# One-hot sets of i: half of them from a table product and ScalarE instead of a VectorE comparison

## The chip, the core and the metric

The kernel runs on one core of a Trainium2 chip. A core has TensorE (PE, matrix products), VectorE (DVE), ScalarE (ACT), GpSimd (POOL) and SyncE (SP, which here issues transfers), and 16 DMA engines that all queues share. The metric is device time in microseconds (us) of one execution, median over runs.

## What is computed

One encoder layer over 1024 tokens of width 1024: attention and a Hyena mixer, a layer norm, and then a PEER feed-forward, which alone matters here. Each token picks, per head, 16 of 128 x 128 experts by the sums of two top-16 lists, and adds the experts' rows up:

```
q = (xc @ w_q).reshape(C, PEER_HEADS, 2, PEER_DK // 2)
s = jnp.einsum('chpd,hpnd->chpn', q, sub_keys, ...)
sv, si = lax.top_k(s, PEER_TOPK)
cand = sv[:, :, 0, :, None] + sv[:, :, 1, None, :]
cidx = si[:, :, 0, :, None] * PEER_NKEYS + si[:, :, 1, None, :]
best, pos = lax.top_k(cand, PEER_TOPK)
eidx = take_along_axis(cidx, pos)
g = softmax(best)
a = gelu(einsum('chkd,cd->chk', u_tab[eidx], xc))
out = einsum('chk,chkd->cd', g * a, v_tab[eidx])
```

An expert's number is 128 i + j, with i and j from 0 to 127.

## The kernel before

The 1024 tokens are eight tiles of 128. Three of them (group 0 to 2) are done by **gathers**: GpSimd fetches the picked rows of peer_u and peer_v by indirect transfers (`grow`, L1249, 128 rows of 4 KB each time, 384 for u and 384 for v), and VectorE makes the dot product of a u row (L1262) or adds a v row up (`gacc`, L1270). Six buffers `grow` go round, so a gather waits for VectorE to have used the row of six before.

The other five tiles are done **densely**: for each of the 128 values of i, TensorE multiplies all 128 experts of that i with the 640 tokens. I call this an expert block. `u_load` fetches the block's table `ur` (512 KB, one buffer), ScalarE rounds it to `uh` (L291) and VectorE makes the rest `ul` (L292), each with two buffers; `u_part` then makes 48 products of 320 columns (L285 to L287) in two banks `ps_x`, and ScalarE takes the gelu of them (L1221) into `A`, which goes to memory in the first 72 blocks (EARLY). Later, `weigh` reads `A` back, multiplies it by the weights `gt`, and `v_group` multiplies by peer_v (`vh`, `vl`): that needs all weights first. So the 72 early blocks and what makes the weights run side by side, and the first v product ends this stage.

Making the weights of a dense tile has two parts. `route` does the top-k lists and finds i, j and the softmax weight, nearly all of it on VectorE; at its end the numbers go through memory (`jx_d`) and come back as `jl`, with tokens along the free side. `build_g` then has 32 steps a tile (160 in all), each for four tokens (NB). A step makes, for each token, a set of one-hots of i (`p1`, a comparison of `iota` with `ig` on VectorE, L1160) and a set of one-hots of j times the weight (`p2`). `p2` comes from a table product, `parabola`: a matmul of `jl` with the constant table `par_r` gives 1-(j-j')^2 in a bank `ps_o` (L1153), and a Relu on ScalarE with the weight as scale leaves the weight where j = j' and zero elsewhere (L1166, one instruction a token). Four matmuls of 128 x 128 a step multiply `p2` by `p1` (L1183; I call them hots), ScalarE copies the result (L1184), and each eight steps go to memory as 2 MB.

The code is written as generators. `weights()` interleaves `route` and `build_g`, and the loop over EARLY takes from it in proportion to the blocks written (`total / GFILL`). The gathers are taken by `tick`. The order on each engine is then chosen by a scheduler from what is ready; only instructions that share buffers are bound to the written order: a pool gives its buffers out in turn, in the order in which the code asks for them. `psX` has four banks, `psH` two, `psO` two (`ps_o0`, `ps_o1`). Before the change only `u_part` asks for banks of `psX` in this stage.

Of the kernel before, what the change touches and what calls it, by code (L numbers as in the profile page):

```python
# [10 lines left out]
F32 = mybir.dt.float32  # L11
F32R = mybir.dt.float32r
BF16 = mybir.dt.bfloat16
I32 = mybir.dt.int32
U32 = mybir.dt.uint32
AF = mybir.ActivationFunctionType
ALU = mybir.AluOpType
# [4 lines left out]
P = 128  # L22
T = 1024
D = 1024
NT = T // P
# [270 lines left out]
def layer(ctx: ExitStack, tc: tile.TileContext, a: dict, out: bass.AP):  # L296
    nc = tc.nc
# [9 lines left out]
    dram = ctx.enter_context(tc.tile_pool(name="dram", bufs=1, space=DRAM))  # L307
# [55 lines left out]
    psX = s_ps.enter_context(tc.tile_pool(name="psX", bufs=4, space=PSUM))  # L363
    psH = s_ps.enter_context(tc.tile_pool(name="psH", bufs=2, space=PSUM))
    psO = s_ps.enter_context(tc.tile_pool(name="psO", bufs=1, space=PSUM))

    def bank():
        return psX.tile([P, 512], F32, name="ps_x")
# [177 lines left out]
    with tc.tile_pool(name="rqp", bufs=1, side="right") as rqp:  # L546
# [4 lines left out]
        for cts, ones in (((0, 1), ones_q), ((2,), ones_kv)):  # L551
# [6 lines left out]
            r = rqp.tile([P, T], F32, name="r")  # L558
# [7 lines left out]
    for j in (*range(4, 12), *range(4)):  # L566
# [5 lines left out]
                                       op0=ALU.mult, op1=ALU.add)  # L572
        nc.vector.scalar_tensor_tensor(y[:, 0:T - 1], u[:, 1:T], sw[:, j, 2:3], y[:, 0:T - 1],
                                       op0=ALU.mult, op1=ALU.add)
# [158 lines left out]
    with tc.tile_pool(name="ltp", bufs=2, side="right") as ltp:  # L733
# [70 lines left out]
        for c in range(2):  # L804
# [6 lines left out]
            for tt in range(0, NT, 2):  # L811
                ps = bank()
                for e in range(2):
                    s = slice((tt + e) * P, (tt + e + 1) * P)
# [110 lines left out]
    iota = keep.tile([P, P], F32, name="iota")  # L925
# [89 lines left out]
    def route(tt, rp, done):  # L1015


        s = rp.tile([P, 16, P], F32, name="r_s")
# [50 lines left out]
        w = rp.tile([P, 8, 16], F32, name="r_w")  # L1069
# [12 lines left out]
        nc.vector.tensor_mul(w, w, den_b)  # L1082
        ei = rp.tile([P, P], I32, name="r_ei")
        nc.vector.tensor_copy(ei, ef2)
        ij = rp.tile([P, 2, P], I32, name="r_ij")
        nc.vector.tensor_scalar(ij[:, 0], ei, 7, None, op0=ALU.arith_shift_right)
        nc.vector.tensor_scalar(ij[:, 1], ei, 127, None, op0=ALU.bitwise_and)
        ijf = rp.tile([P, P], F32, name="r_ijf")
        nc.vector.tensor_copy(ijf, ij[:, 0])
        jj = rp.tile([P, P], I32, name="r_jj")  # L1090
        nc.vector.tensor_tensor(jj, ij[:, 1], ij[:, 1], op=ALU.mult)
        jp = rp.tile([P, 2, P], I32, name="r_jp")
        nc.vector.tensor_scalar(jp[:, 1], jj, 127, None, op0=ALU.bitwise_and)
        nc.vector.tensor_scalar(jp[:, 0], jj, 127 << 7, None, op0=ALU.bitwise_and)
        jx = rp.tile([P, 3, P], BF16, name="r_jx")
        nc.vector.tensor_copy(jx[:, 0], ij[:, 1])
        nc.vector.tensor_copy(jx[:, 1:3], jp)
        nc.sync.dma_start(jx_d[tt].rearrange("r t s -> t r s"), jx)
        jl = jls[tt % 2]
        for r in range(3):  # L1100
            nc.sync.dma_start(jl[32 * r:32 * r + 32], jx_d[tt, r].rearrange("(q t) s -> t q s", t=32))
        ps = psO.tile([P, 2, P], F32, name="ps_o0")
        nc.tensor.transpose(ps[:, 0], ijf, ident)
        nc.tensor.transpose(ps[:, 1], w.rearrange("p h k -> p (h k)"), ident)
        ig = rp.tile([P, 2, P], F32, name="ig", bufs=2)
# [28 lines left out]
    CS = 32  # L1134
    GI = 4
    NCS = TD // CS
    jx_d = dram.tile([NT, 3, P, P], BF16, name="jx_d")
    NB = 4
    HOT = 0.69
    g_d = dram.tile([NCS, P, P, CS], F32, name="g_d")  # L1140
# [1 line left out]
    def build_g(ijg, t, gp):  # L1142


        ig, jl = ijg
        steps = [(cs, c4) for cs in range(P // CS) for c4 in range(0, CS, NB)]
        par, hot = {}, {}

        def parabola(n):
            cs, c4 = steps[n]  # L1150
            ps = psO.tile([P, NB, P], F32, name=f"ps_o{n % 2}")
            c = cs * CS + c4
            nc.tensor.matmul(ps, jl[0:98, c // 32], par_r[0:98, c % 32:c % 32 + NB], start=True, stop=True)  # L1153
            par[n] = ps

        def hots(n):
            cs, c4 = steps[n]
            c = cs * CS + c4
            p1 = gp.tile([P, NB, P], F32, name="p1", bufs=4)
            nc.vector.tensor_tensor(p1, iota.unsqueeze(1).to_broadcast([P, NB, P]),  # L1160
                                    ig[:, 0, c:c + NB].unsqueeze(2).to_broadcast([P, NB, P]),
                                    op=ALU.is_equal)
            p2 = gp.tile([P, NB, P], F32, name="p2", bufs=4)
            ps = par.pop(n)
            for j in range(NB):
                nc.scalar.activation(p2[:, j], ps[:, j], AF.Relu, scale=ig[:, 1, c + j:c + j + 1])  # L1166
            hot[n] = p1, p2

        with tc.issue_after(ended[-1]) if ended else ExitStack():
            parabola(0)  # L1170
            parabola(1)
        hots(0)
        for n, (cs, c4) in enumerate(steps):
            if n + 2 < len(steps):
                parabola(n + 2)
            if n + 1 < len(steps):
                hots(n + 1)
            if c4 == 0:
                st = gp.tile([P, P, CS], F32, name="gst", bufs=2)
            p1, p2 = hot.pop(n)  # L1180
            ps = psH.tile([P, NB, P], F32, name="ps_h")
            for j in range(NB):
                nc.tensor.matmul(ps[:, j], p2[:, j], p1[:, j], start=True, stop=True)  # L1183
            nc.scalar.copy(st[:, :, c4:c4 + NB], ps.rearrange("p c i -> p i c"))  # L1184
            if c4 + NB == CS:
                nc.scalar.dma_start(g_d[t * (P // CS) + cs], st)
            yield HOT
# [20 lines left out]
    def u_part(i, psum):  # L1208

        for n in (i, i + 1):  # L1210
            if n < P and n not in ready:
                u_load(n)
        uh, ul = ready.pop(i)
        A = up.tile([P, TD], F32, name="A", bufs=3)
        for c in range(2):
            s = slice(c * HT, (c + 1) * HT)
            ps = psum()
            for ct in range(ND):
                r = mm3(nc, ps, (uh[:, ct], ul[:, ct]), (hd[:, 0, ct, s], hd[:, 1, ct, s]),
                        ct == 0, ct == ND - 1)  # L1220
            nc.scalar.activation(A[:, s], ps, AF.Gelu)  # L1221
        ended.append(r.ins)
        return A
# [71 lines left out]
    def tick(cost):  # L1295
        pace["credit"] += cost
        while pace["credit"] >= pace["step"]:
            pace["credit"] -= pace["step"]
            next(ga, None)
# [5 lines left out]
    with tc.tile_pool(name="rp", bufs=1, side="left") as rp, \  # L1305
            tc.tile_pool(name="gp", bufs=1, side="left") as gp:
        base = gp.tile([98, P], F32, name="base")
        own = gp.tile([98, 32], F32, name="own")
        nc.sync.dma_start(base, a["par_base"])
        nc.sync.dma_start(own, a["par_own"])  # L1310
        par_r = gp.tile([98, 32, P], BF16, name="par_r")
        nc.vector.tensor_mul(par_r, base.unsqueeze(1).to_broadcast([98, 32, P]),
                             own.unsqueeze(2).to_broadcast([98, 32, P]))
        jls = [gp.tile([98, 4, P], BF16, name=f"jl{i}") for i in range(2)]
        for jl in jls:
            nc.gpsimd.memset(jl[96:98], 1.0)
        r0 = route(0, rp, [])
        for _ in scores(hd, NG, DENSE):
            with tc.issue_after(normed[-1].ins):
                for _ in range(2):  # L1320
                    next(r0, None)
        for _ in r0:
            pass
        s_q.close()
        gap = s_e.enter_context(tc.tile_pool(name="gap", bufs=2, side="right"))

        def weights():


            done = []  # L1330
            yield from route(NG, rp, done)
            for t in range(DENSE):
                beside = route(NG + t + 1, rp, done) if t + 1 < DENSE else route(1, rp, done)
                for n, c in enumerate(build_g(done[t], t, gp)):
                    yield c
                    if n % 5 in (0, 2, 4):
                        yield next(beside, 0.0)
                yield from beside
            for g in range(2, NG):
                yield from route(g, rp, done)  # L1340

        gw = weights()
        total = (NT - 1) * 12 * CHUNK + TD // NB * HOT
        done = 0.0
        for e in range(EARLY):
            while done < (e + 1) * total / GFILL:
                c = next(gw, None)
                if c is None:
                    break
                done += c  # L1350
            A = u_part(e, u_early)
            nc.scalar.dma_start(a_d[e], A)
            tick(UC)
        for _ in gw:
            pass
# [199 lines left out]
```

## Time and profile before

| | |
|---|---|
| three runs | 3267.38 us median (3263.86 to 3277.91) |
| the profiled execution | 3255.75 us, span 3254.0 us |
| TensorE busy | 2988.5 us (92%) |
| VectorE busy | 2735.7 us (84%) |
| ScalarE busy | 1256.2 us (39%) |
| GpSimd busy | 1036.4 us (32%) |

Busy time is the union of an engine's instructions. A matmul's recorded length covers the length of its pipeline, and the next one starts well before its end, so a busy TensorE is not a full one: its true load is read from the distance of starts. Idle time of an engine matters only where others wait for it.

### The profile page before, as it was taken

The numbers are of one execution on the slowest core, as the hardware profiler recorded it, in microseconds if no ns is written. First come the engines' busy times: TensorE is split into PE (matmuls) and PEld (weight loads), VectorE is DVE, ScalarE is ACT, GpSimd is POOL, SyncE is SP. The second block draws the span as 40 slices with busy tenths as digits, with TensorE's granted clock in tenths as the row PEclk, the third lists the DMA queues.
The fourth block names the chain that finished last, engine by engine and source line by source line (L and its number), as shares of the span: only waits on it lengthen the run. The fifth ranks groups of instructions, "written<-read, shape, count | busy, mean of one in ns | idle before, by whom it ended". The sixth has DMA issues, their size and how long they took to land.

```text
span 3254.0 us, 44798 instructions
## 1 busy us (share of the span) xinstructions
PE 2988.5 (92%) x15582; PEld 2552.1 (78%) x15582; DVE 2735.7 (84%) x5514; ACT 1256.2 (39%) x2454; POOL 1036.4 (32%) x797
## 2 busy tenths in 40 slices
PE   6999898889999779999999789998999999799997
PEld 5677676556689778999898778886888888588886
DVE  7556799888757799999999768888889879888888
ACT  4544344455523216766574122222222222122222
POOL 0000000000000351332435735555555445455551
PEclk9999889989999989999999899999999999999998
DMA  5244743322444777887888999999999999989995
GB/s 173 97 149 133 249 123 104 102 56 73 138 152 149 278 252 241 302 303 277 310 284 319 364 338 336 325 358 341 329 358 323 353 315 333 337 302 353 342 332 188
DMA packets 355064, 828.87 MB, mean 255 GB/s; under 512 B 34345, under 2 KB 144851, under 8 KB 351253
## 3 DMA queue, kind: packets, MB, share of 16 engines
q0 software_dynamic: 110592, 402.70, 34.5%
q1 hardware_dynamic: 230709, 356.71, 33.9%
q10 hardware_dynamic: 13536, 66.59, 5.2%
q8 instruction: 123, 2.02, 0.2%
q14 instruction: 104, 0.85, 0.1%
HBM read 715.52 MB, written 110.33 MB: 254 GB/s over the span
## 4 chain that ended last, share of the span: by engine, by line
PE 31%; DVE 22%; DMA 7%; issue 6%; POOL 3%; ACT 1%; SPq 0%; DVEq 0%; POOLq 0%; ACTq 0%
PE ps_x L285 5%; PE ps_x L287 5%; PE ps_x L286 5%; DVE grow L1262 4%; DVE gacc L1270 4%; DMA vr<-in_peer_v 3%; PE ps_h L285 3%; PE ps_h L287 3%; PE ps_h L286 3%; POOL grow L1249 3%; DVE p L1160 2%; PE ps_o L285 2%; PE ps_o L286 2%; PE ps_o L287 2%; DVE ul L292 2%
## 5 line engine op out<-in xcount | busy, mean ns | idle before, releaser
L1249 POOL DMA_INDIRECT grow<-in_peer_u,eid x384 | 518.0, 1349 | 582.3 <-DVE grow L1262 206.9
L1249 POOL DMA_INDIRECT grow<-in_peer_v,eid x384 | 504.8, 1315 | 606.1 <-DVE gacc L1270 267.3
L1270 DVE SCALAR_TENSOR_TENSOR gacc<-grow,dot,gacc 128x1024 f32<-128x1024 f32 x381 | 487.3, 1279 | 13.2 <-DMA grow<-in_peer_v,eid 9.6
L1262 DVE SCALAR_TENSOR_TENSOR grow<-grow,gh 128x1024 f32<-128x1024 f32 x384 | 460.1, 1218 | 19.8 <-DMA grow<-in_peer_u,eid 19.5
L287 PE MATMUL ps_x<-hd,ul 128*128 128x320 f32 x1152 | 368.3, 328 | 50.1 <-DVE ul L292 49.7
L285 PE MATMUL ps_x<-hd,uh 128*128 128x320 f32 x1152 | 373.6, 325 | 28.4 <-ACT uh L291 26.2
L286 PE MATMUL ps_x<-hd,uh 128*128 128x320 f32 x1152 | 370.3, 322 | 0.0
L286 PE MATMUL ps_x<-vl,wh 128*128 128x512 f32 x864 | 341.1, 395 | 1.7 <-DVE vl L292 1.6
L287 PE MATMUL ps_x<-vh,wl 128*128 128x512 f32 x864 | 336.8, 393 | 0.0
L285 PE MATMUL ps_x<-vh,wh 128*128 128x512 f32 x864 | 302.3, 396 | 28.4 <-ACT vh L291 23.2
L291 ACT CAST vh<-vr 128x512 fp32r<-128x512 f32 x256 | 156.3, 619 | 388.4 <-DMA vr<-in_peer_v 280.6
L285 PE MATMUL ps_h<-hd,uh 128*128 128x320 f32 x896 | 278.8, 311 | 9.0 <-ACT A L1221 5.6
L286 PE MATMUL ps_h<-hd,uh 128*128 128x320 f32 x896 | 278.3, 311 | 0.0
L287 PE MATMUL ps_h<-hd,ul 128*128 128x320 f32 x896 | 275.8, 311 | 2.5 <-DVE ul L292 2.5
L287 PEld LDWEIGHTS ps_x<-hd,ul 128*128 128x128 f32 x1152 | 222.7, 195 | 65.0 <-DVE ul L292 59.0
L285 PEld LDWEIGHTS ps_x<-hd,uh 128*128 128x128 f32 x1152 | 225.9, 196 | 35.4 <-ACT uh L291 31.8
L292 DVE TENSOR_TENSOR vl<-vr,vh 128x512 fp32r<-128x512 f32 x256 | 174.5, 687 | 75.7 <-ACT vh L291 74.4
L286 PEld LDWEIGHTS ps_x<-hd,uh 128*128 128x128 f32 x1152 | 225.8, 196 | 0.8
L291 ACT CAST uh<-ur 128x1024 fp32r<-128x1024 f32 x128 | 134.7, 1052 | 223.7 <-DMA ur<-in_peer_uT 103.1
L285 PEld LDWEIGHTS ps_x<-vh,wh 128*128 128x128 f32 x864 | 162.7, 190 | 63.5 <-ACT vh L291 24.7
L292 DVE TENSOR_TENSOR ul<-ur,uh 128x1024 fp32r<-128x1024 f32 x128 | 155.5, 1215 | 63.8 <-ACT uh L291 62.4
L286 PEld LDWEIGHTS ps_x<-vl,wh 128*128 128x128 f32 x864 | 164.4, 190 | 37.1 <-DVE vl L292 4.4
(366 smaller groups left out, 6876.3 us busy)
## 6 DMA issues: line engine op xcount, KB each, us to landing
ur<-in_peer_uT SPq DMA_DIRECT2D x128, 512.0 KB
vr<-in_peer_v SPq DMA_DIRECT2D x256, 256.0 KB
g_d<-gst ACTq DMA_DIRECT2D x20, 2048.0 KB
gt<-g_d SPq DMA_DIRECT2D x32, 1280.0 KB
a_d<-A ACTq DMA_DIRECT2D x72, 320.0 KB
A<-a_d SPq DMA_DIRECT2D x72, 320.0 KB
fw<-in_dft_fw SPq DMA_DIRECT2D x64, 256.0 KB
wr<-in_w_in SPq DMA_DIRECT2D x16, 512.0 KB
```

The lines of the kernel that those rows point to most:

```text
L285: nc.tensor.matmul(out, L[0], R[0], start=start, stop=False)
L286: nc.tensor.matmul(out, L[0], R[1], start=False, stop=False)
L287: return nc.tensor.matmul(out, L[1], R[0], start=False, stop=stop)
L291: nc.scalar.copy(hi, src)
L292: return nc.vector.tensor_sub(lo, src, hi)
L1160: nc.vector.tensor_tensor(p1, iota.unsqueeze(1).to_broadcast([P, NB, P]), ig[:, 0, c:c + NB].unsqueeze(2).to_broadcast([P, NB, P]), op=ALU ...
L1249: nc_i = nc.gpsimd.indirect_dma_start(out=t, out_offset=None, in_=a["peer_" + kind], in_offset=bass.IndirectOffsetOnAxis(ap=eid[g][:, k:k ...
L1262: nc.vector.scalar_tensor_tensor(t, t, 1.0, h_t, op0=ALU.mult, op1=ALU.mult, accum_out=d[:, k - k0:k - k0 + 1])
L1270: nc.vector.scalar_tensor_tensor(acc, t, dots[k0][:, k - k0:k - k0 + 1], acc, op0=ALU.mult, op1=ALU.add)
```

## The change

In every second step of `build_g`, `p1` no longer comes from the comparison. `route` sends three rows more through memory (i beside j, its square's high and low part), so `x_d` has six rows for three and `jl` two halves; there are six loads for three. In a step with odd number `parabola` makes a second product with the same table from the half of i, in a bank taken from `psX`, and one Relu on ScalarE of 128 x 512 turns it into `p1`. In an even step the comparison stays.

```diff
-        ij = rp.tile([P, 2, P], I32, name="r_ij")
-        nc.vector.tensor_scalar(ij[:, 0], ei, 7, None, op0=ALU.arith_shift_right)
...
+        nc.vector.tensor_tensor(x2, xx[:, 0], xx[:, 0], op=ALU.mult)
+        nc.vector.tensor_scalar(xx[:, 1], x2, 127 << 7, None, op0=ALU.bitwise_and)
+        nc.vector.tensor_scalar(xx[:, 2], x2, 127, None, op0=ALU.bitwise_and)
+        xb = rp.tile([P, 6, P], BF16, name="r_xb")
+        nc.vector.tensor_copy(xb, xx.rearrange("p r w s -> p (r w) s"))
+        nc.sync.dma_start(x_d[tt].rearrange("r t s -> t r s"), xb)
+        jl = jls[tt % 2]
+        for r in range(6):
+            nc.sync.dma_start(jl[32 * (r // 2):32 * (r // 2) + 32, r % 2],
+                              x_d[tt, r].rearrange("(q t) s -> t q s", t=32))
...
-            ps = psO.tile([P, NB, P], F32, name=f"ps_o{n % 2}")
             c = cs * CS + c4
-            nc.tensor.matmul(ps, jl[0:98, c // 32], par_r[0:98, c % 32:c % 32 + NB], start=True, stop=True)
-            par[n] = ps
+            par[n] = []
+            for w in range(n % 2 == 0, 2):
+                ps = psO.tile([P, NB, P], F32, name=f"ps_o{n % 2}") if w else psX.tile([P, NB, P], F32, name="ps_x")
+                nc.tensor.matmul(ps, jl[0:98, w, c // 32], par_r[0:98, c % 32:c % 32 + NB], start=True, stop=True)
+                par[n].append(ps)
...
+            *pi, pj = par.pop(n)
+            if pi:
+                nc.scalar.activation(p1, pi[0], AF.Relu)
+            else:
+                nc.vector.tensor_tensor(p1, iota.unsqueeze(1).to_broadcast([P, NB, P]),
+                                        ig[:, 0, c:c + NB].unsqueeze(2).to_broadcast([P, NB, P]),
+                                        op=ALU.is_equal)
```

The change moves instructions well beyond the edited lines. Three places follow. The number behind a name tells how early the code, as written, asked for that buffer. First, TensorE at the first parabola of the first dense tile, before:

```order
L286 MATMUL ps_x_10142<-hd_7120,uh_10003 128x320
L1153 LDWEIGHTS jl1_7577
L1153 MATMUL ps_o0_9033<-par_r_7574,jl1_7577 128x512
L1153 LDWEIGHTS jl1_7577
L1153 MATMUL ps_o1_9035<-par_r_7574,jl1_7577 128x512
L287 MATMUL ps_x_10142<-hd_7120,ul_10004 128x320
```

The blocks' banks (10142) are there far ahead of the parabolas that were written before them (9033, 9035): blocks had run past the weights. The same place now:

```order
L287 MATMUL ps_x_8964<-hd_7120,ul_8861 128x320
L1102 MATMUL ps_o0_9029<-ident_60,r_ijf_9027 128x128
L1103 MATMUL ps_o0_9029<-ident_60,r_w_9002 128x128
L1154 LDWEIGHTS jl1_7577
L1154 MATMUL ps_x_9036<-par_r_7574,jl1_7577 128x512
L285 MATMUL ps_x_9089<-hd_7120,uh_8933 128x320
```

The banks of `psX` now follow one another in the order written, 8964, 9036 (the new parabola of i), 9089. Ahead of the first hot stand 811 block products before (16.9 blocks) and 375 now (7.8); ahead of the first v product stand 3648 in both (76 blocks).

Second, VectorE at the 55th `ul` of 128, before (the two ends of what stands between two of them):

```order
L292 TENSOR_TENSOR ul_15099<-ur_15096,uh_15098 128x1024
L1262 SCALAR_TENSOR_TENSOR grow_15371,dot_15257<-grow_15371,gh_8448 128x1024
L1050 MAX_INDEX r_pos_16556<-r_best_16555,r_cand_16538 128x8 x2
L1160 TENSOR_TENSOR p1_15528<-iota_6486,ig_14576 128x512
L1160 TENSOR_TENSOR p1_15563<-iota_6486,ig_14576 128x512
L1160 TENSOR_TENSOR p1_15578<-iota_6486,ig_14576 128x512
L1262 SCALAR_TENSOR_TENSOR grow_15374,dot_15257<-grow_15374,gh_8448 128x1024
```

And now:

```order
L1274 SCALAR_TENSOR_TENSOR gacc_8450<-grow_18064,dot_17570,gacc_8450 128x1024
L1166 TENSOR_TENSOR p1_15425<-iota_6486,ig_14699 128x512
L1284 SCALAR_TENSOR_TENSOR gacc_8450<-gh_8448,gacc_8450 128x1024
L328 BN_STATS ln_st_18171<-gacc_8450 128x6 x2
L292 TENSOR_TENSOR ul_15238<-ur_15235,uh_15237 128x1024
L330 BN_AGGR ln_mv_18174<-ln_st_18171 128x2
L333 RECIPROCAL ln_rs_18176<-ln_rs_18176 128x1
L292 TENSOR_TENSOR ul_15339<-ur_15336,uh_15338 128x1024
L1166 TENSOR_TENSOR p1_15543<-iota_6486,ig_14699 128x512
L292 TENSOR_TENSOR ul_15457<-ur_15454,uh_15456 128x1024
```

Between the ninth `ul` and the 55th VectorE now has all 112 dot products and all 122 `gacc` of the stage's remaining gathers, all of the routes and 69 comparisons; before, it had 72, 73 and 139, and the rest of the gathers came behind. After the 55th `ul` only 21 more `ul`, 11 comparisons and a few small ones are left for VectorE up to the first v product.

Third, ScalarE in the first dense tile, now; before, there is no row like the third, and `gst` and `p2` alternate:

```order
L1188 COPY gst_9541<-ps_h_9796 128x128x4
L1170 ACTIVATE p2_9898<-ps_o0_9802,ig_9032 128x128 x4
L1188 COPY gst_9541<-ps_h_9811 128x128x4
L1164 ACTIVATE p1_9912<-ps_x_9893 128x512
L1170 ACTIVATE p2_9913<-ps_o1_9895,ig_9032 128x128 x4
```

The new Relu stands between the copies and the old ones.

## Rows read from the trace of the kernel before

**Rows 1.** Busy time of each engine in six stretches and the rest, from the stage's ninth `ul`.

```profile
core 0: us, PE busy (x) PEld busy (x) DVE busy (x) ACT busy (x) POOL busy (x), PEclk, DMA share, GB/s
1149.00:1243.00 94.00, 71.07 (x429) 68.45 (x428) 94.00 (x311) 21.45 (x39) 45.75 (x28) 0.89 0.75 251
1243.00:1520.00 277.00, 266.94 (x1903) 256.87 (x1902) 276.15 (x822) 183.82 (x508) 79.02 (x67) 0.99 0.81 288
1520.00:1687.00 167.00, 158.23 (x1114) 152.38 (x1114) 167.00 (x512) 109.07 (x302) 54.71 (x42) 0.98 0.80 287
1687.00:1775.00 88.00, 81.69 (x569) 76.92 (x568) 84.26 (x160) 53.35 (x145) 44.99 (x29) 0.98 0.89 315
1775.00:1890.00 115.00, 88.14 (x520) 82.40 (x518) 90.70 (x110) 21.16 (x35) 80.89 (x62) 0.93 0.98 370
1890.00:1931.00 41.00, 30.43 (x188) 29.12 (x188) 19.23 (x22) 11.86 (x18) 6.44 (x5) 0.94 0.89 291
1931.00:3254.00 1323.00, 1262.46 (x6336) 1095.19 (x6336) 1143.62 (x1551) 343.62 (x569) 678.20 (x508) 0.98 0.93 327
```

**Rows 2.** Timeline of TensorE (start, length): products of a block, hots, parabola, first v.

```profile
1243.37 0.83 PE L1183 MATMUL ps_h<-p,p 128*128 128x128 f32 x6
1244.03 0.38 PE L1153 MATMUL ps_o<-par_r,jl 98*128 98x512 bf16 x1
1244.25 0.83 PE L1183 MATMUL ps_h<-p,p 128*128 128x128 f32 x6
...
1400.31 0.31 PE L286 MATMUL ps_x<-hd,uh 128*128 128x320 f32 x1
1400.46 0.31 PE L287 MATMUL ps_x<-hd,ul 128*128 128x320 f32 x1
...
1431.28 1.05 PE L1183 MATMUL ps_h<-p,p 128*128 128x128 f32 x8
1432.09 0.39 PE L287 MATMUL ps_x<-hd,ul 128*128 128x320 f32 x1
...
1931.02 2.07 PE L285 MATMUL ps_x<-vh,wh 128*128 128x512 f32 x4 [5.68 <-ACT vh L291]
```

**Rows 3.** Timeline of VectorE: ninth and 55th `ul`, a dot product, a comparison and a `gacc`.

```profile
1148.78 1.20 DVE L292 TENSOR_TENSOR ul<-ur,uh 128x1024 fp32r<-128x1024 f32 x1
...
1448.08 1.22 DVE L1262 SCALAR_TENSOR_TENSOR grow<-grow,gh 128x1024 f32<-128x1024 f32 x1
1449.23 0.69 DVE L1160 TENSOR_TENSOR p<-iota,ig 128x512 f32<-128x512 f32 x1
1449.83 1.28 DVE L1270 SCALAR_TENSOR_TENSOR gacc<-grow,dot,gacc 128x1024 f32<-128x1024 f32 x1
...
1686.85 1.21 DVE L292 TENSOR_TENSOR ul<-ur,uh 128x1024 fp32r<-128x1024 f32 x1
```

**Rows 4.** The whole stretch 1149 to 1931 in one, same columns as group 1.

```profile
1149.00:1931.00 782.00, 696.50 (x4714) 666.14 (x4712) 731.34 (x1931) 400.72 (x1041) 311.79 (x231) 0.96 0.84 298
```

**Rows 5.** Lines L1184 and L1160: ns min/median/max, first and last start.

```profile
L1184 ACT COPY gst<-ps_h x160: 570/602/829, 1245.5 to 1773.8; 128x512 f32<-128x512 f32 x160
L1160 DVE TENSOR_TENSOR p<-iota,ig x160: 628/675/694, 1230.7 to 1765.5; 128x512 f32<-128x512 f32 x160
```

**Rows 6.** Preparing `jl`: the transfers, and the last cast before them.

```profile
L1101 SPq DMA_DIRECT2D jl<-jx_d x15: 325/426/1263, 1233.3 to 1641.6; - x15
...
L1097 DVE CAST r_jx<-r_jp x5: 263/264/273, 1230.6 to 1637.0; 128x256 bf16<-128x256 int32 x5
```

**Rows 7.** Waits between 1243 and 1687 (total us, times, longest).

```profile
POOL grow L1249 <- DVE gacc L1270: 81.5, 18, 10.8
...
ACT uh L291 <- DMA ur<-in_peer_uT: 35.1, 14, 5.9
```

**Rows 8.** The gathers' DMA queue, and three kinds of transfer with their sizes.

```profile
q0 software_dynamic: 110592, 402.70, 34.5%
...
ur<-in_peer_uT SPq DMA_DIRECT2D x128, 512.0 KB
...
g_d<-gst ACTq DMA_DIRECT2D x20, 2048.0 KB
...
a_d<-A ACTq DMA_DIRECT2D x72, 320.0 KB
```

More of the change, by code (lines that the diff above doesn't have):

```diff
@@ L1084, in route @@
         nc.vector.tensor_copy(ei, ef2)
-        ij = rp.tile([P, 2, P], I32, name="r_ij")
-        nc.vector.tensor_scalar(ij[:, 0], ei, 7, None, op0=ALU.arith_shift_right)
-        nc.vector.tensor_scalar(ij[:, 1], ei, 127, None, op0=ALU.bitwise_and)
-        ijf = rp.tile([P, P], F32, name="r_ijf")
[L1089 to L1101, printed above, removed]
+        xx = rp.tile([P, 3, 2, P], I32, name="r_xx")
+        nc.vector.tensor_scalar(xx[:, 0, 0], ei, 7, None, op0=ALU.arith_shift_right)
+        nc.vector.tensor_scalar(xx[:, 0, 1], ei, 127, None, op0=ALU.bitwise_and)
+        x2 = rp.tile([P, 2, P], I32, name="r_x2")
+        nc.vector.tensor_tensor(x2, xx[:, 0], xx[:, 0], op=ALU.mult)
[8 more added lines that the diff above has]
+                              x_d[tt, r].rearrange("(q t) s -> t q s", t=32))
+        ijf = rp.tile([P, P], F32, name="r_ijf")
+        nc.vector.tensor_copy(ijf, xx[:, 0, 0])
         ps = psO.tile([P, 2, P], F32, name="ps_o0")
@@ L1136, in layer @@
     NCS = TD // CS
-    jx_d = dram.tile([NT, 3, P, P], BF16, name="jx_d")
+    x_d = dram.tile([NT, 6, P, P], BF16, name="x_d")
     NB = 4
@@ L1159, in hots @@
             p1 = gp.tile([P, NB, P], F32, name="p1", bufs=4)
-            nc.vector.tensor_tensor(p1, iota.unsqueeze(1).to_broadcast([P, NB, P]),
-                                    ig[:, 0, c:c + NB].unsqueeze(2).to_broadcast([P, NB, P]),
-                                    op=ALU.is_equal)
             p2 = gp.tile([P, NB, P], F32, name="p2", bufs=4)
-            ps = par.pop(n)
+            *pi, pj = par.pop(n)
[5 more added lines that the diff above has]
+                                        op=ALU.is_equal)
             for j in range(NB):
-                nc.scalar.activation(p2[:, j], ps[:, j], AF.Relu, scale=ig[:, 1, c + j:c + j + 1])
+                nc.scalar.activation(p2[:, j], pj[:, j], AF.Relu, scale=ig[:, 1, c + j:c + j + 1])
             hot[n] = p1, p2
@@ L1313, in layer @@
                              own.unsqueeze(2).to_broadcast([98, 32, P]))
-        jls = [gp.tile([98, 4, P], BF16, name=f"jl{i}") for i in range(2)]
+        jls = [gp.tile([98, 2, 4, P], BF16, name=f"jl{i}") for i in range(2)]
         for jl in jls:
```

## The prediction, made before the changed kernel ran

> **What bounds it now.** I read the busy times by stretch first, since the change touches one stage alone, the one in which weights are made beside the early blocks. From 1149 us on VectorE is busy without a gap for 94 us, then for 276 of 277 and 167 of 167 us [rows 1]: until 1687 us this stage goes at VectorE's pace. TensorE's busy column reads almost the same (267 of 277), but there it deceives: a block's product is recorded with 0.31 us and the next starts after 0.147 us [rows 2]. By starts, a block of 48 products costs 7.06 us, a step's four hots (8 records) 0.81 us and a parabola 0.22 us [rows 2]. Between the first hot (1243.4) and the first v product (1931.0) lie 3648-811 = 2837 block products, 640 hots and some 158 parabolas: 417+130+35 = 582 us of work in 688 us. TensorE is 85% full there, and has a hundred microseconds of slack.
>
> The last part of the stage has another limit. From 1775 to 1890 us VectorE is busy for 91 of 115 us, but DMA stands at 0.98 and 370 GB/s [rows 1]: the gathers that VectorE was late with are fetched flat out. GpSimd's longest wait before that is for `gacc` to free a row buffer, 81.5 us [rows 7]. So the stage is VectorE's, with a piece of work put off to its end that keeps DMA full.
>
> **What the change removes.** 80 of 160 comparisons. One is recorded with 0.675 us [rows 5]; the next instruction starts after 0.60 us (1449.23 to 1449.83) [rows 3]. That is 80 x 0.60 = 48 us off VectorE.
>
> **What it adds.** TensorE gets 80 parabolas, 80 x 0.22 = 18 us. ScalarE gets 80 Relus of 128 x 512 out of PSUM. The trace has none; the nearest row is the copy of the same shape out of PSUM, 0.602 us [rows 5], which gives 48 us. Below it stands nothing, above it twice that price. ScalarE is busy for 401 of 782 us [rows 4], and 183.8 of 277 in its fullest stretch [rows 1], so I cost it at nothing; without that cover it is 48 us. One of the skill's rules speaks against this move. The Trainium skill ("ScalarE: Activation LUTs", Rules for kernel authors) tells to give Relu to VectorE, which it calls up to about three times faster per element in bf16. Here the comparison works on fp32, and rows 5 have both engines level, so the trace does not bear the rule out for this shape; by the rule a Relu would cost some 1.8 us, 144 us in all, which ScalarE's idle time would still hold.
>
> `route` computes with twice or three times the columns: five dense tiles, one product and two masks of 256 columns, one cast of 768. The cast of 256 takes 0.264 us [rows 6]; at three times that, and the other three doubled at most, a tile costs 0.5 to 1.3 us more, 3 to 6 us in all, of which I take 3. There are three more loads a tile on SP's queue at 0.426 us [rows 6], 1.3 us a tile, behind which the next `ur` stands; SP is held for it anyway by the write before, so between 0 and 6 us, and I take 0.
>
> If nothing else moved, VectorE would gain 45 us.
>
> **What else moves.** The order listed ahead shows more than that. (It is that of a fresh build; the traced program follows its own list row for row to about the 20th `ul`, then shifts by a few rows.) The new parabolas take banks of `psX` in turn with the blocks, and the blocks can no longer run past the weights: 7.8 blocks stand ahead of the first hot, where 16.9 did. These nine blocks, 436 products or 64 us, now come later, while the first hot itself needs the same routes as before and moves by a few microseconds. Between the first hot and the first v, TensorE now has 3273 products, 640 hots and 237 parabolas: 481+130+52 = 663 us, 81 more.
>
> VectorE keeps busy meanwhile with what is ready: gathers and routes. That is the second place in the order: by the 55th `ul` VectorE has done all 112 dot products, all 122 `gacc` and every route. Since it takes its list in order, the 55th `ul` can't come before them. The stretch 1149 to 1931 holds 731 us of VectorE's work [rows 4]. Take off the 48, add 3 for `route`, and take off what the list puts behind the 55th `ul`: 22 `ul` at 1.15 us (25; the price is that of a dot product of the same width, by starts 1448.08 to 1449.23 [rows 3]), 11 comparisons (7) and 3 us of small ones. That leaves 651 us, so the 55th `ul` can't start before 1149+651 = 1800 us; in the trace it starts at 1687 [rows 3].
>
> Behind it TensorE has 22 blocks, 100 hots and 31 parabolas up to the first v: 1056 x 0.147 = 155, 20 and 7, together 182 us, 186 at the granted clock of 0.98 [rows 1], with VectorE nearly idle. These two pieces now come one after the other; before, the last gathers and the last blocks ran side by side.
>
> DMA adds some. Between the 40th and 55th `ul` the list has 92 gathered rows. A gather is 402.7 MB / 768 = 0.524 MB; with 15 `ur` and `a_d`, and six writes of 2 MB [rows 8], this is 48+13+13 = 74 MB. VectorE's own work between the two is 92 x 1.17 for the gathers, 15 x 1.15, 24 comparisons at 0.60 and some 47 us of routes, 187 us, which asks for 394 GB/s; the fullest stretch moved 370 [rows 1], so it takes 200: 13 us more. From nothing to 21 (if the traffic before is late too), I take 10. The wait in front of the first v product, 5.7 us for `vh` [rows 2], stays.
>
> The sum: 1800+10+1 (`ul` to TensorE)+186+6 = 2003 us for the first v product, against 1931: 72 us later. What comes behind, 1323 us [rows 1], has the same instructions and the same gathers left (group 0 is done and group 1 not begun in either list), so it stays. Against the profiled execution, 3255.75+72 = 3328; its time lies 11.6 us under the median of the runs, and to that I add the same 72: 3339 us, 2.2% slower. About 0.5%, 16 us, is what a measurement of this kernel can tell from no change.
>
> A rule of the skill bears on the mechanism: the Trainium skill ("Trainium Kernel Development and Optimization", Best Practices) says that regular bubbles can mean that PSUM has run out. By it the gaps on TensorE would come from banks; in the trace of before the waits are for `ul` and `uh`, and no run here shows the changed kernel's yet.
>
> **The rivals.**
>
> TensorE sets the stage, and VectorE's list doesn't. If the `ul` come in time, the 663 us count alone; at the 0.95 that TensorE reached by starts while full (a block product of 0.147 us at a clock of 0.98 to 0.99, few waits), that is 698 us, a first v at 1941, and 3277 us. For it: the slack of 51 us that VectorE has in 782 [rows 4], and that a build can place gathers elsewhere. Against: the list.
>
> Faster: the nine held-back blocks are made up for at full rate, the `ul` come ahead of the gathers' work, and the flat-out gathers at 1775 to 1890 are gone since VectorE is never late. Then TensorE's work is the floor: 1243+663 = 1906, 25 us earlier, 3242 us. That VectorE's whole 45 us be had is excluded by this floor. It decides itself at the 55th `ul`: with 186 behind it, it must start before 1906-186 = 1720 us for a gain. The list has it behind 651 us of work, which speaks against.
>
> That the change doesn't do what it says is a small rival: if ScalarE's Relus come late, VectorE has 48 us less and the hots still wait. From 1243 to 1687 it is busy for 293 of 444 us [rows 1], and 151 idle against 48 more speak against that; it would look like the forecast's time with the waits on ScalarE instead, and I give it no chance of its own.
>
> **Chances and range.** The late 55th `ul` 0.70, with 54 to 100 us (DMA's term 0 to 21, VectorE's sum 4% smaller as listings of before overstate it, or ScalarE and SP's terms 10): 3321 to 3367 us. TensorE alone 0.14, 3260 to 3283 us. Faster 0.10. Something slower yet milder or heavier 0.06. By 0.5%: faster 0.10, same 0.13, slower 0.77. The range from 3277 to 3375 leaves out the faster case and half of TensorE's.
>
> **What would show it.** Right: some eight blocks ahead of the first hot, where there were 17; VectorE's `ul` 55 near 1800 to 1810 and all `gacc` of group 0 before it; the comparisons 80, ScalarE 45 to 55 us busier; a stretch of some 180 us before the first v in which VectorE, GpSimd and DMA are nearly idle and TensorE works on blocks alone; the first v near 2000 and 1320 us behind it. Wrong: a first v before 1950; `gacc` still running beside the last blocks; or ScalarE as what TensorE waits for.

## The result, and the profile after

The changed kernel took 3349.4 us (median of four runs, 3337.2 to 3353.3) against 3265.6 us in the same comparison: a ratio of 1.0243, 95% interval 1.0205 to 1.0282. The profiled execution took 3346.65 us, 91 us more than that of before. The forecast was 3339 us.

Busy time by stretch, after; the columns are those of [rows 1].

```profile
1149.00:1243.00 94.00, 8.21 (x42) 7.50 (x43) 94.00 (x340) 5.47 (x14) 38.95 (x30) 0.52 0.61 192
1243.00:1520.00 277.00, 257.33 (x1758) 242.41 (x1757) 269.98 (x875) 170.94 (x449) 93.90 (x72) 0.96 0.80 281
1520.00:1687.00 167.00, 148.62 (x961) 135.81 (x961) 153.95 (x378) 95.22 (x259) 81.13 (x62) 0.95 0.87 313
1687.00:1850.00 163.00, 136.70 (x833) 122.65 (x832) 133.08 (x221) 82.83 (x220) 90.90 (x69) 0.87 0.91 335
1850.00:2035.00 185.00, 181.36 (x1258) 177.77 (x1257) 38.39 (x42) 82.34 (x184) 0.00 (x0) 1.00 0.52 175
2035.00:3344.00 1309.00, 1259.74 (x6335) 1091.50 (x6334) 1142.53 (x1550) 343.39 (x568) 680.86 (x508) 0.99 0.94 331
```

Two things are new. In the first stretch TensorE is busy for 8 of 94 us, where it was for 71. In the fifth, 185 us long, TensorE is full (181) while VectorE has 38 us of work, GpSimd none, and DMA is half idle: TensorE works on alone. What lies behind the first v product is nearly as long as before (1309 and 1323 us). The timeline of TensorE shows the first stretch's cause, and the first v product.

```profile
1216.17 0.47 PE L1102 MATMUL ps_o<-ident,r_ijf 128*128 128x128 f32 x1 [79.68 <-DVE r_ijf L1100]
...
1235.48 0.59 PE L1154 MATMUL ps_x<-par_r,jl 98*128 98x512 bf16 x1 [18.62 <-DMA jl<-x_d]
...
1236.40 0.47 PE L287 MATMUL ps_x<-hd,ul 128*128 128x320 f32 x1
1236.66 0.47 PE L285 MATMUL ps_x<-hd,uh 128*128 128x320 f32 x1
...
1239.56 0.31 PE L286 MATMUL ps_x<-hd,uh 128*128 128x320 f32 x1
1239.71 0.31 PE L287 MATMUL ps_x<-hd,ul 128*128 128x320 f32 x1
...
2034.19 2.08 PE L285 MATMUL ps_x<-vh,wh 128*128 128x512 f32 x4 [3.10 <-ACT vh L291]
```

TensorE stands for 79.7 us at the transposes that end the first dense tile's `route`, since VectorE is still busy with routes, and for 34 us of it with gathered rows. Then it stands for 18.6 us more, until `jl` is there. Of these, VectorE takes 9.8 to finish the six rows (L1093), among other work of its list; the way through memory takes the 8.8 us from that cast's end at 1226.66 to the product at 1235.48:

```profile
1226.12 0.55 DVE L1093 CAST r_xb<-r_xx 128x768 bf16<-128x768 int32 x1
...
1226.69 0.38 SPq L1094 DMA_DIRECT2D x_d<-r_xb  x1
1229.78 2.71 SPq L1097 DMA_DIRECT2D jl<-x_d  x6
```

Before, blocks filled most of this time. The same stretch from 1136 us on, before and after, and TensorE's only listed wait in it before:

```profile
1136.00:1243.00 107.00, 79.39 (x473) 76.78 (x474) 107.00 (x369) 23.74 (x43) 48.56 (x31) 0.87 0.73 240
1136.00:1243.00 107.00, 8.70 (x46) 7.73 (x45) 107.00 (x394) 8.55 (x18) 41.76 (x33) 0.54 0.61 189
...
PE ps_x L287 <- DVE ul L292: 27.7, 9, 6.9
```

The 55th `ul` of VectorE, with what precedes and follows it:

```profile
1837.88 6.57 DVE L1274 SCALAR_TENSOR_TENSOR gacc<-grow,dot,gacc 128x1024 f32<-128x1024 f32 x5
1845.66 1.22 DVE L292 TENSOR_TENSOR ul<-ur,uh 128x1024 fp32r<-128x1024 f32 x1 [1.21 <-ACT uh L291]
1846.80 1.22 DVE L1284 SCALAR_TENSOR_TENSOR gacc<-gh,gacc 128x1024 f32<-128x1024 f32 x1
```

The last `gacc` of group 0 stand right ahead of it, as listed. And the two ways to a set of one-hots of i, 80 each (ns min/median/max, first and last start):

```profile
L1164 ACT ACTIVATE p<-ps_x x80: 578/643/892, 1236.1 to 1930.5; 128x512 f32<-128x512 f32 x80
L1166 DVE TENSOR_TENSOR p<-iota,ig x80: 659/680/695, 1221.4 to 1928.5; 128x512 f32<-128x512 f32 x80
```

### The profile page after: what moved, and what is told of

The parts are those of the page before. It is cut to its first block, busy times and chain, and to the rows that moved or that the text cites. A ratio compares the mean times of both kernels' runs of the same rounds, so it can differ in the third digit from the quotient of the medians.

```text
span 3344.9 us, 44966 instructions
## 1 busy us (share of the span) xinstructions
PE 3016.1 (90%) x15662; PEld 2559.5 (77%) x15662; DVE 2691.2 (80%) x5429; ACT 1291.6 (39%) x2532; POOL 1032.1 (31%) x797
## 4 chain that ended last, share of the span: by engine, by line
PE 55%; DVE 21%; DMA 14%; issue 5%; ACT 3%; POOL 2%; SPq 1%; DVEq 0%; ACTq 0%; POOLq 0%
PE ps_x L285 10%; PE ps_x L287 9%; PE ps_x L286 9%; DMA vr<-in_peer_v 5%; PE ps_h L285 3%; PE ps_h L286 3%; PE ps_h L287 3%; DVE grow L1266 3%; DMA ur<-in_peer_uT 3%; PE ps_o L285 2%; PE ps_o L286 2%; DVE gacc L1274 2%; PE ps_o L287 2%; DMA grow<-in_peer_u,eid 2%; POOL grow L1253 2%
## 5 line engine op out<-in xcount | busy, mean ns | idle before, releaser
L287 PE MATMUL ps_x<-hd,ul 128*128 128x320 f32 x1152 | 368.7, 327 | 27.7 <-DVE ul L292 27.7
L285 PE MATMUL ps_x<-hd,uh 128*128 128x320 f32 x1152 | 376.6, 327 | 18.5 <-ACT uh L291 18.5
```

The costliest lines, as they stand in the source:

```text
L285: nc.tensor.matmul(out, L[0], R[0], start=start, stop=False)
L287: return nc.tensor.matmul(out, L[1], R[0], start=False, stop=stop)
```

## The experiments

The theory: banks of `psX`, handed out in the written order, hold the blocks behind the first dense tile's weights; VectorE then does the gathers first, and the last blocks run alone. Rivals: the Relus on ScalarE, the 18 us of products on TensorE, or `route`'s six rows and loads.

"First v" is the start of the first v product, "stand" TensorE's wait at the first transposes and then for `jl`, "ahead" the block products that the trace has before the first hot, by 48.

| kernel | us, median | first v | stand | ahead |
|---|---|---|---|---|
| before, profiled / built anew (e6) | 3265.6 / 3273.9 | 1931.0 / 1939.8 | 0 / 0 | 16.9 / 16.9 |
| changed, profiled / built anew (e10) | 3349.4 / 3355.8 | 2034.2 / 2040.7 | 79.7+18.6 / 80.8+18.3 | 7.8 / 7.8 |
| e1: bank of i from psH | 3297.6 | 1949.1 | 0 | 17.3 |
| e2: lock alone | 3340.2 | 2026.3 | 80.8+18.5 | 7.4 |
| e4: nine blocks asked first | 3276.8 | 1953.2 | 6.4+18.5 | 15.8 |
| e8: five blocks asked first | 3301.1 | 1981.2 | 42.5+19.8 | 12.8 |
| e5: preparation alone | 3275.4 | 1946.2 | 0 | 17.1 |
| e7: relief alone | 3262.4 | 1945.6 | 0 | 16.9 |
| e9: before, nine asked first | 3268.0 | 1942.5 | 0 | 18.0 |
| e11: lock in first tile only | 3330.3 | 2006.4 | 80.9+18.6 | 7.8 |
| e12: gathers written later | 3377.7 | 2055.3 | 57.7+13.4 | 7.8 |
| e13: all sets from the table | 3318.4 | 1999.8 | 6.5+17.5 | 15.8 |

In the three comparisons of the experiments, the kernel before took 3296 to 3297 us, each time on another chip, 0.9% more than in the first one, and a new build of the same source 3274. What differs between these builds is not known. The ratios below are against the 3296 to 3297; I lean on times beside those of e6 and e10, and above all on the first v, and read nothing from 1% between two builds.

**The bank elsewhere (e1).** The new products, Relus and loads stay; only the bank's pool changes.

```diff
-... if w else psX.tile([P, NB, P], F32, name="ps_x")
+... if w else psH.tile([P, NB, P], F32, name="ps_h")
```

> The changed kernel with one difference: the parabola of i takes its bank from psH, which the hots use, and not from psX. The Relus on ScalarE, the 80 more products on TensorE, the 80 comparisons fewer on VectorE and the six loads all stay. Theory (banks of psX handed out in written order hold the blocks back): blocks run ahead of the first hot again as far as before (about 17, for 7 to 8 in the changed kernel), TensorE's 80 us stand at the transposes of the first dense tile is gone, and the time is that of the kernel before or a little better, 3225 to 3270 us. Rival (ScalarE's 80 Relus, or the 18 us of products more on TensorE, or the six loads are what costs): all of these are still there, so 3320 to 3355 us.

Ratio 1.0004 (0.9991 to 1.0016), 3297.6 us, first v at 1949.1. The stand is gone and 17.3 blocks run ahead. The time is above the range given; the stretch behind the first v, 1345 us in its 3294.6 us span, is 20 to 35 us longer than in the other kernels (1311 to 1326), which I can't explain. But ScalarE's Relus, TensorE's 80 products and the six loads are all there, and the first v is 85 to 92 us earlier than with the bank in `psX`. They are not what costs.

**The lock alone (e2).** The kernel before, with an unread product into a bank of `psX` in odd steps; all comparisons stay.

```diff
+            if n % 2:
+                px = psX.tile([P, NB, P], F32, name="ps_x")
+                nc.tensor.matmul(px, jl[0:98, c // 32], par_r[0:98, c % 32:c % 32 + NB], start=True, stop=True)
```

> The kernel before with one thing added: in odd steps a second product of the old rows of jl goes into a bank of psX, and nobody reads it. No Relu is added, all 160 comparisons stay on VectorE, three loads a tile as before. Theory (written order of psX's banks): about 7 to 8 blocks ahead of the first hot, TensorE stands still for 70 to 90 us at the first dense tile, VectorE's 48 us are not taken off, so at least the time of the changed kernel: 3340 to 3400 us. Rival (ScalarE, route's new work or the six loads): only 18 us of products are added where TensorE has a hundred of slack, so 3262 to 3285 us.

Ratio 1.0131 (1.0109 to 1.0154), 3340.2 us; the waits of TensorE (total us, times, longest) between 1140 and 1260:

```profile
PE ps_o L1103 <- DVE r_ijf L1089: 80.8, 1, 80.8
PE ps_o L1156 <- DMA jl<-jx_d: 18.5, 1, 18.5
```

The lock makes the stand and a first v at 2026 by itself. Two more points: the 18.5 us until `jl` is there come with three loads as with six; and this kernel is not slower than the changed one, though VectorE still has its 48 us. I had said "at least the time of the changed kernel". So nothing of the relief is seen at the end even where the stage is late. That is no clean price of it, since the order differs too: ahead of the 55th `ul` (1826.8) this kernel has 28 gathered rows fewer (116 dot products and 111 `gacc`, for 128 and 127), and VectorE waits 20 us up to there, where in the changed kernel it waits 50.

**Blocks asked for earlier (e4, five blocks: e8).** The changed kernel; the bank stays in `psX`. In e8 both 9 are 5.

```diff
-            while done < (e + 1) * total / GFILL:
+            while done < (e + 1 - 9) * total / (GFILL - 9):
```

> The changed kernel, where the code asks for nine blocks before it takes the first piece of weights' work, and spreads that work over the 62 blocks that follow. The parabola of i keeps its bank in psX. Theory (written order): the written order now itself puts about 16 blocks ahead of the first hot, so the banks no longer hold them back and most of the loss is regained: 3230 to 3285 us, TensorE's 80 us stand gone. Rival (ScalarE's Relus, TensorE's added products, route's preparation): nothing of these is changed, so 3330 to 3355 us. Third possibility: the bank is held by the Relu of i all through the stage and slows the blocks even then; that would give 3290 to 3330 us.

> The changed kernel where the code asks for five blocks before the first piece of weights' work (nine in the experiment before, none in the changed kernel). Theory (what the written order puts ahead of the first hot sets the loss): about 12 to 13 blocks ahead, TensorE's stand at the first dense tile 35 to 50 us for 80, a first v product between the two others, 1970 to 2010, and a ratio of 1.005 to 1.015, between 1.0243 and 0.9952. Rival (any earlier asking cures it, by some other way than the lead): 0.993 to 1.000.

e4: ratio 0.9952 (0.9936 to 0.9967), 3276.8 us, in the theory's range, though 25 us of the stand are left. e8: 1.0016 (1.0000 to 1.0032), 3301.1 us. By time, e8 lies between the two others as the theory wants, though its ratio is under the range, which I had set by the first comparison's build; beside e6's 3273.9 us it is 1.008, inside. In the table first v follows the stand: 98, 62 and 25 us of it give 2034, 1981 and 1953. The step between the two is there as well: the 55th `ul` starts at 1846 us in the changed kernel, 1827 in e2, 1762 in e8, 1726 in e4 and 1720 in e1, against 1687 and 1705 (e6) in the kernel before. The written order's lead sets the loss.

**The preparation alone (e5).** Only `route`'s part of the change.

```diff
-            for w in range(n % 2 == 0, 2):
+            for w in range(1, 2):
```

> Of the change only route's part: six rows through memory, six loads for three, the doubled integer work on VectorE. No parabola of i, no Relu of i; all 160 comparisons are on VectorE. Theory: this costs 3 to 6 us of VectorE's time in a stage that goes at its pace, 3263 to 3276 us, which is no change that can be measured. Rival (the six loads on SP's queue delay the tables, or the 18.6 us wait for jl in the changed kernel is their price): 3285 to 3350 us.

Ratio 0.9946 (0.9926 to 0.9966), 3275.4 us, as the new build of before (3273.9). It costs nothing that can be measured.

**Before, built anew (e6).** No edit.

> The kernel before, unchanged, built anew: a control. On the chip of the first four experiments the kernel before took 3296 us, against 3266 elsewhere, and the stretch behind the first v product was between 1309 and 1341 us long there for the same instructions. Ratio 1.000 within 0.003 if a fresh build is the same program. If a fresh build places gathers otherwise, 0.99 to 1.01, and then no single ratio between these bounds says anything of an edit. The stretch behind the first v product by its profile: 1310 to 1345 us.

Ratio 0.9926 (0.9905 to 0.9947), 3273.9 us. A ratio against the comparison's own build is off by that much.

**The relief alone (e7).** The kernel before, without the odd steps' comparisons.

```diff
-            p1 = gp.tile([P, NB, P], F32, name="p1", bufs=4)
...
+            if n % 2:
+                p1 = last[0]
+            else:
...
+                last[0] = p1
```

> The kernel before without 80 of its 160 comparisons: an odd step takes the one-hots of i of the step before it, so its weights are those of other rows of the table. Nothing is put in their place: no product, no Relu, no bank, three loads. It prices the 48 us that the change takes off VectorE, by themselves. Reading A (the stage goes at VectorE's pace to its end): the first v product 40 to 48 us earlier, about 1888, and a ratio of 0.985 to 0.988. Reading B (behind VectorE stands the next limit, the transfers of the last gathers and then TensorE's work): the first v between 1915 and 1945, a ratio of 0.993 to 1.002, VectorE idle 40 us more between 1687 and 1850 us, waiting for gathered rows or for uh.

Ratio 0.9892 (0.9869 to 0.9915), 3262.4 us: 11 us under e6, with a first v at 1945.6, no earlier than e6's 1939.8. The ratio lies between the two readings' ranges; beside e6 it is 0.9965, in reading B's, and the first v is at the edge of B's 1945. So reading B is the nearer one. The windows of the relief alone (columns as above), around where VectorE's time would have to turn into an earlier end:

```profile
1520.00:1687.00 167.00, 146.57 (x964) 136.72 (x963) 157.99 (x477) 87.13 (x231) 73.08 (x48) 0.94 0.82 288
1687.00:1850.00 163.00, 145.39 (x952) 135.31 (x951) 125.90 (x149) 75.32 (x204) 99.29 (x73) 0.96 0.95 356
```

The same of before, built anew:

```profile
1520.00:1687.00 167.00, 152.23 (x1057) 144.66 (x1056) 166.78 (x517) 103.96 (x282) 52.88 (x43) 0.97 0.80 285
1687.00:1850.00 163.00, 141.48 (x939) 135.79 (x938) 141.39 (x230) 71.72 (x184) 93.56 (x66) 0.94 0.92 333
```

VectorE has 9 and 15 us less work in these two stretches, and ends no earlier for it: GpSimd fetches gathers earlier (73 us of work for 53), and then DMA goes to 0.95 and VectorE idles for 37 of 163 us (22 in e6: 15 more, where reading B had 40). VectorE is not what the stage waits for once it is relieved. The order differs as well: 96 dot products and 84 `gacc` stand ahead of the 55th `ul` in e7, for 88 and 79 in e6, and it starts at 1720.2 for 1704.8; so the price is that of the relief in its own order.

**Before, blocks asked for earlier (e9).** The edit of e4 on the kernel before.

> The kernel before, with the code asking for nine blocks before the first piece of weights' work, as in the experiment on the changed kernel: is that ratio of 0.9952 due to the table product or to the earlier asking? Theory: in the kernel before the blocks run ahead in any case (about 17 to 18 blocks), so the asking gives next to nothing, 0.995 to 1.003. If the earlier asking itself is what gains, 0.985 to 0.994, and the table product costs the difference.

Ratio 0.9899 (0.9877 to 0.9922), 3268.0 us, 6 us under e6 with a first v at 1942.5. The ratio itself lies in the range of the second reading, that the asking gains; but e6, with no edit at all, has 0.9926, and beside e6 it is 0.998, in the theory's. Against the new build the asking gives next to nothing. So e4's 0.9952 is no gain either, and no kernel here is shown to beat the one before.

**The changed kernel built anew (e10).** No edit.

> The changed kernel, unchanged, built anew: a control, since a new build of the kernel before came out 0.7% faster than the build that it is compared with. 3320 to 3355 us, first v product at 2010 to 2040 us, the 55th rounding rest of a block's table at 1820 to 1850 us.

Ratio 1.0172 (1.0145 to 1.0199), 3355.8 us, first v at 2040.7, the 55th `ul` at 1851, each just above its range. Beside e6 it is 2.5%.

**The lock in the first tile only (e11).** Tiles 1 to 4 take their banks of i from `psH`.

```diff
-... if w else psX.tile([P, NB, P], F32, name="ps_x")
+... if w else (psH if t else psX).tile([P, NB, P], F32, name="ps_h" if t else "ps_x")
```

> The changed kernel, in which only the first dense tile's parabolas of i take banks of psX; those of the other four tiles take psH. If the loss is made once, when TensorE stands at the first dense tile's transposes and nine blocks fall behind: lead 7 to 8 blocks, stand about 80 us, 3320 to 3355 us, first v product 2010 to 2040 us as in the changed kernel. If it builds up tile by tile (the blocks held back at each tile's first parabola): a fifth of the loss, 3280 to 3300 us, first v product 1945 to 1975 us.

Ratio 1.0097 (1.0071 to 1.0124), 3330.3 us, first v at 2006.4. Between e1 (1949.1) and e10 (2040.7) lie 92 us; the first tile alone makes 57 of them. Neither reading's range has this first v. So most of the loss is made once, and the four later tiles add 34, which two builds of the changed kernel (2034 and 2041) leave uncertain by some 7.

**Gathers written later (e12).** To take work from VectorE ahead of the 55th `ul`.

```diff
-            tick(UC)
+            if e < 8:
+                tick(UC)
```

> The changed kernel, in which the code asks for gathers only beside the first eight of the 72 early blocks and for the rest behind them. By the listed order VectorE then has 97 dot products and 96 sums of group 0 ahead of the 55th ul, where it had 128 and 128: 74 us of work less. If VectorE's list is what sets the 55th ul, it starts at 1765 to 1785 us for 1845, and the first v product comes at 1960 to 1990 us for 2034, although the banks are handed out as in the changed kernel and 7 to 8 blocks stand ahead of the first hot. If TensorE's stand alone sets the end (nine blocks that are not made up for), the first v stays at 2015 to 2040 us. The whole time says less, since gathers are moved behind the stage: 3270 to 3350 us.

Ratio 1.0241 (1.0216 to 1.0267), 3377.7 us. The list's part came out: the 55th `ul` starts at 1777.7, in the range. The end didn't follow: first v at 2055, later than both readings. The gathers that left the place ahead of the 55th `ul` came behind it, with the next group's (some 30 dot products and as many sums more before the first v), as the window behind it shows:

```profile
1850.00:2055.00 205.00, 155.28 (x918) 144.90 (x917) 145.39 (x177) 55.51 (x115) 128.18 (x94) 0.88 0.99 365
```

DMA is full at 365 GB/s, and TensorE is no longer alone. Here the 55th `ul` didn't set the end, with gathers left behind it.

**All sets from the table (e13).** All 160, with e4's earlier asking.

```diff
-            for w in range(n % 2 == 0, 2):
+            for w in range(2):
```

> All 160 sets of one-hots of i from the table product and ScalarE, none compared on VectorE, the bank in psX, and the code asking for nine blocks before the weights' work, as in the experiment that gave 3277 us. VectorE loses another 48 us, TensorE and ScalarE get another 18 and 48. Reading B of the relief (VectorE's time is worth nothing behind the next limit): 3270 to 3300 us, first v product 1945 to 1980 us. Reading A (VectorE's time counts): 3225 to 3250 us, first v near 1905.

Ratio 1.0060 (1.0038 to 1.0083), 3318.4 us, first v at 1999.8. Both readings miss. It is 47 us later than e4, for 18 us more of TensorE's products. VectorE's waits between 1149 and 1850 (total us, times, longest) show one part:

```profile
DVE ul L292 <- ACT uh L291: 41.4, 11, 7.7
DVE gacc L1274 <- DMA grow<-in_peer_v,eid: 17.3, 9, 5.2
```

The first was 4.5 us in e4. Whether ScalarE's Relus or the shared banks make `uh` late was not tried.

## Why the prediction was right

**The lock.** As told: 7.8 blocks ahead of the first hot for 16.9. e1 (bank elsewhere: gone) and e2 (lock alone: there) show it, and e4 and e8 that it goes by the lead. I had counted nine blocks of TensorE's time, 64 us. The trace has 436 block products fewer ahead of the first hot, as counted, and between 1136 and 1243 TensorE is busy 71 us less. The stand is 98 us, because it also holds the 27.7 us for which before TensorE waited there for `ul`. The last 18.6 of it, up to `jl`, I hadn't listed; before, blocks hid them. Somewhat over a third of the loss comes from the later tiles (e11, 34 of 92 us).

**VectorE's sum.** 651 us ahead of the 55th `ul`, forecast; the first four windows after add up to 94.0+270.0+154.0+133.1 = 651.0 us up to 1850, so some 647 up to the 55th `ul`. `route`'s integer work went from 9.3 to 11.1 us by its groups, 1.8 us for the 3 taken. The Relu took 0.643 us beside the 0.602 taken, and ScalarE's busy time rose by 35 us (45 to 55 forecast); e1 shows it hidden there. This bears on the rule I had cited from the Trainium skill ("ScalarE: Activation LUTs", Rules for kernel authors): ScalarE's Relu takes 0.643 us where VectorE's comparison takes 0.680 for a set of the same size. But the rule is on a Relu, with its figure in bf16, and no run here has a Relu on VectorE; so the runs neither bear it out nor speak against it, and my sentence on it said more than the rows do.

**The transfers' term: mis-sized.** I took 10 us (0 to 21) of VectorE's waiting before the 55th `ul`, which therefore should have come at 1810; it came at 1845.7. The waits between 1243 and 1850, after (total us, times, longest):

```profile
ACT uh L291 <- DMA ur<-in_peer_uT: 38.3, 16, 6.7
...
DVE ul L292 <- ACT uh L291: 22.1, 10, 4.8
...
DVE grow L1266 <- DMA grow<-in_peer_u,eid: 16.1, 9, 4.4
...
DVE gacc L1274 <- DMA grow<-in_peer_v,eid: 5.8, 3, 4.9
```

VectorE waits 50 us in all up to the 55th `ul`, and 44 of them are these: 22 for gathered rows and 22 for `uh`. The second part is not all a transfer's. Ahead of four of its ten waits (13 us) ScalarE had just waited for `ur` from memory; ahead of the other six (9 us) it came from other work, such as the gelu of a block. One of each:

```profile
1593.66 1.04 ACT L291 CAST uh<-ur 128x1024 fp32r<-128x1024 f32 x1 [6.66 <-DMA ur<-in_peer_uT]
...
1707.72 0.44 ACT L1225 ACTIVATE A<-ps_x 128x320 f32<-128x320 f32 x1 [2.79 <-PE ps_x L287]
...
1708.61 1.04 ACT L291 CAST uh<-ur 128x1024 fp32r<-128x1024 f32 x1 [0.45 <-ACT A L1225]
```

So at most 35 us stand against the term's 10. At least 9 came by way of ScalarE's own list, which I had costed at nothing, and some 5 are small waits. Of the 44 us, 30 lie between the 40th `ul` and the 55th, where I had looked for the rush:

```profile
1622.00:1846.00 224.00, 189.44 (x1185) 170.19 (x1185) 188.97 (x315) 121.49 (x331) 124.39 (x93) 0.91 0.90 329
```

VectorE's 189 us of work there are the 187 forecast, and 224 us at 329 GB/s are the 74 MB forecast. The rate was wrong: I had put the 370 GB/s of the fullest stretch.

**The end alone.** 193 us from the 55th `ul` to the first v, forecast; 1845.7 to 2034.2 are 188.5, with VectorE nearly and GpSimd wholly idle; DMA, which I had forecast nearly idle too, was at 0.52. The first v was thus 31 us later than the 2003 forecast: 36 from the 55th `ul`, less 5 here. The rest, 1311 us to the span's end for 1323, gave 12 back. 31-12 = 19 us is what the profiled execution's 3346.65 differs from 3328. That the time came so close is in part luck: the first v came 103 us after before's, above the 54 to 100 that I had given this case, and nothing had forecast the 12 us that the rest gave back.

**What the relief was worth.** The sum took 48 us off for the comparisons, as if time off VectorE came off the end. Its own 651 us came out; but e7 gives at most 11 us at the end for the 48, none before the first v, and e2 keeps the 48 us and ends no later. It looks like the same error as the waits' term, seen from the other side: up to the 55th `ul` VectorE waits 50 us, where in e2, with the 48 us more to do, it waits 20. But the orders of the two differ, so how much of the relief went into waits isn't shown. The rival "faster" had the wrong ceiling, not only the wrong chance: relieved and with nothing held back, the first v came at 1946 (e7) and 1949 (e1), not at TensorE's 1906. In the other rival, TensorE's 0.95 by starts is high: for 1243 to 1520 of before, the same prices give 253 of 277 us, 0.91.

**Banks as the cause of gaps.** The Trainium skill ("Trainium Kernel Development and Optimization", Best Practices) has regular bubbles as a possible sign that PSUM has run out. Here the loss is for the most part a single stand put down to `r_ijf`, and no row names a bank; only the runs (e1, e2, e4) show that a bank's pool is behind it. And e4 regains most of it with the same banks in another written order, so what bound here was the order in which they are handed out. The rule's sign is not there, and that PSUM ran out is not what these runs show.

## What to carry to other kernels

A buffer taken from a pool that others use in turn binds their order: before a step borrows a bank, see which work was running ahead because nobody else asked for that pool (here nine blocks and 2.4% of the time), and take the bank elsewhere or write the code so that the lead stands in its order. An engine that is busy without a gap need not be worth relieving: leave the work out once and see what the end gains (here 11 us at most of 48). Two builds of one source differed by 0.7% here in one comparison, so build the kernel before anew before reading a change smaller than that.

## What the runs showed of the hardware that was not expected

The way of `jl` through memory, one write and its loads, takes 8.8 us in the changed kernel, from the end of the last cast to the first product. With three loads it is no shorter to speak of: 8.3 us in e2 (1231.62 to 1239.92) and 9.0 in before (1230.82 to 1239.83), where blocks hide it. After the stand TensorE's products started 0.26 us apart (1236.40 to 1236.66) and from about 1239 on 0.15 us; the granted clock of that stretch was 0.52, near the lower of its two levels, for 0.89 before. With a dozen products at that pace it cost under 2 us.
